# Order of the first loads, statistics ahead of the modulation, and the modulation on four column tiles, in a hybrid pool and state-space block

## The chip, the cores and the metric

The kernel runs on one core of a Trainium2 chip. The metric is the device time of one execution in microseconds. A core has five engines that run beside each other and meet at semaphores: TensorE (PE in the rows, its weight loads PEld), VectorE (DVE), ScalarE (ACT), GpSimd (POOL) and SyncE (SP), which issues most loads. ScalarE issues DMAs as well.

## The reference

One layer of a hybrid block with depth 1: 2048 latent tokens and 256 context tokens of width 1024. Both are normalised and modulated, projected by `w_in`, and fed to a pooling mixer and a bidirectional state-space mixer, whose outputs meet in `w_out`. Cut to what matters here:

```python
mod_lat = silu(c) @ w_ada + b_ada              # 1024 -> 3 x 1024
mod_ctx = silu(c_ctx) @ w_ada + b_ada
sh, sc, g = split(mod, 3)
hm = rmsnorm(h, norm_w) * (1 + sc) + sh        # for the context and for the latents
p  = hm @ w_in                                  # x/B/C columns, dt, gates, pool branch
# conv, chunked scans, box means, gates, then
h = h + g * (concat(y_pool, y_ssd) @ w_out);  out = rmsnorm(h, final_norm_w)
```

The pooling branch's per-group linear map (`pool_w`) is multiplied into its input projection: `s_wp` is that product, 256 x 1024 for each of four groups.

## The kernel before

Activations lie transposed, with channels on the 128 partitions and tokens along the free dimension: 8 chunks of channels, latents in four blocks of 512 tokens (`hm0` to `hm3`), the context in one of 256 (`hc`). Each is kept as a rounded part and a remainder, and each projection is three matmuls per chunk k (`project`).

The start of the program, up to line 460, is what the change touches. It does these things:

- *Modulation.* Eight chunks of `w_ada` (128 rows x 2048 columns, 1 MiB each, `ada`) are multiplied with `scol`, the silu of both condition vectors (2 columns per chunk): four matmuls of 128x2 by 128x512 per chunk into four banks `pm0` to `pm3`, two rows of each. Four copies (`mrow`), sixteen small transposes into `pmc`, and the bias give `mod` (shift and scale by channel) and `acol`, (1 + scale) times the norm's weight.
- *Statistics* (`Tokens.squares`, `mean`, `spread`). ScalarE squares eight chunks, GpSimd and VectorE add them up, TensorE sums over partitions (`ms`), a chain of small operations on VectorE and ScalarE forms the reciprocal root, ScalarE spreads it on a diagonal (`dg`), and TensorE makes a row block of it (`rstd`).
- *Modulation of the tokens* (`Tokens.modulate`). For each chunk VectorE forms `tt` (line 197), ScalarE the rounded part (line 199), VectorE the remainder (line 202), of `hc` for the context and `hm` for a latent block.
- *Pool maps* 0 and 1 (`pool_map`). TensorE forms eight pieces `pw`, ScalarE copies them, and issues two stores to `s_wp`.
- *Column tiles 0 and 1.* `pc` is the context's projection, `px` a latent block's, `pdt` the projection for dt. Weights come as `wraw_x`, are rounded by ScalarE (line 213), and the remainder is formed by GpSimd (line 214).

From column tile 2 on, a regular loop over 14 tiles follows, and then the other stages.

Three things set the order. Every engine works through its own list in order. A scheduler that works from estimated times makes these lists from the order of the program, so lines can move against each other. And each DMA, whichever engine issues it, takes the next of eight completion counters in turn (named DMAHW0 to DMAHW7 in the order's rows); an issue waits until the counter's previous DMA, the one eight places earlier, has landed. This wait stands in the list of the engine that issues.

Tiles with the tag `slot` share four large buffers: a fifth tile takes the buffer of one that is no longer read.

Of the kernel before, what the change touches and what calls it, by code (L numbers as in the profile page):

```python
# [23 lines left out]
def hybrid_block(ctx, tc, d, out):  # L24
    nc = tc.nc
    P = 128
# [24 lines left out]
    def mm(o, l, r, start, stop):  # L51
        nc.tensor.matmul(o, l, r, start=start, stop=stop)  # L52
# [28 lines left out]
    ident = const("ident", [P, P])  # L81
# [6 lines left out]
    mod = const("mod", [P, 16, 2])  # L88
    acol = const("acol", [P, 8, 2])
    scol = const("scol", [P, 8, 2])  # L90

    def exp_table(after):
        with tc.issue_after(after.ins):
            nc.scalar.preload_act_table_set("natural_log_exp_and_others")

    exp_table(nc.scalar.activation(scol, ccol, AF.Silu))

    def rsqrt(pool, ms, n, nm):
        v = pool.tile([P, n], F32, tag="rv", name=f"rv{nm}")
# [30 lines left out]
        return dg  # L130


    def ada_rows(ps, wa, k, who):

        for j, p in enumerate(ps):
            mm(p[0:who.stop - who.start, :], scol[:, k, who], wa[:, j * 512:(j + 1) * 512], k == 0, k == 7)

    class Tokens:

# [66 lines left out]
    def raw_weights(src, nm):  # L206
        raw = rpool.tile([P, 8, P], F32, tag="wraw", name=f"wraw_{nm}")
        nc.sync.dma_start(raw, src)
        return raw

    def split_weights(raw, nm, eng=nc.gpsimd):
        w = wpool.tile([P, 2, 8, P], F32R, tag="w", name=f"w_{nm}")
        nc.scalar.copy(w[:, 0], raw)
        eng.tensor_tensor(w[:, 1], raw, w[:, 0].bitcast(F32), op=ALU.subtract)
        return w
# [106 lines left out]
    wd = dp.tile([P, 8, P], F32R, tag="wd", name="wd")  # L322
    ctxt = Tokens(hc, 256, d["ctxT"], 1, "c", wpool.tile([P, 8, 256], F32, tag="w", name="xc"))
    ada = [slot(f"ada{a}", [P, 4, 2048], F32) for a in range(2)]
    cu = slot("cu", [P, 8192], F32)
    hm, tok = [], []

    def latent(b, raw=None):
        tok.append(Tokens(None, 512, d["xT"][b], 0, f"l{b}", raw, (4, 4, 6, 6)[b]))
        if raw is not None:  # L330
            tok[b].load()
# [2 lines left out]
        tok[b].h = slot(f"hm{b}", [P, 2, 8, 512], F32R)  # L334
        hm.append(tok[b].h)

    hm0 = slot("hm0", [P, 2, 8, 512], F32R)
    xs = slot("xs", [P, 2, 8, 512], F32)

    def pool_map(g, ks):  # L340
        uT = cu[:, 2048 * g:2048 * g + 2048].rearrange("p (a b) -> p a b", a=2)
        wl = cu[:, 4096 + 512 * g:4608 + 512 * g].rearrange("p (a b) -> p a b", a=2)
        wo = cu[:, 5120:7168] if g == 0 else cu[:, 0:2048]
        wo = wo.rearrange("p (k t) -> p k t", k=8)
        if 0 in ks:
# [15 lines left out]

    cols = [Columns(ct) for ct in range(16)]

    for k in range(4):
        load_ada(k)
    draw = rpool.tile([P, 8, 32], F32, tag="wraw", name="draw")
    nc.sync.dma_start(draw, d["w_dt"])
    ctxt.load()
    for k in range(4, 8):
        load_ada(k)  # L370
    norm_w = const("norm_w", [P, 8], d["norm_w"], pool=dp)
    b_mod = const("b_mod", [P, 16], d["b_mod"], pool=dp)
    conv_w = const("conv_w", [P, 16, 4], d["conv_w"], pool=dp)
    conv_b = const("conv_b", [P, 16], d["conv_b"], pool=dp)
    dtb_row = const("dtb_row", [P, 32], d["dt_bias"].broadcast_to([P, 32]), pool=dp)
    a_row = const("a_row", [P, 32], d["a_log"].broadcast_to([P, 32]), pool=dp)
    pool_map(0, (0,))
    latent(0, xs[:, 0])
    hm.append(hm0)
    tok[0].h = hm0  # L380
    raws = [raw_weights(d["w_xbc"][0], "x0")]
    pool_map(1, (0,))
    raws.append(raw_weights(d["w_xbc"][1], "x1"))
    nc.vector.memset(wd.bitcast(F32), 0.0)
    nc.vector.tensor_copy(wd[:, :, 0:32], draw)
    nc.vector.tensor_tensor(wd[:, :, 32:64], draw, wd[:, :, 0:32].bitcast(F32), op=ALU.subtract)
    pm = [pp(f"pm{j}") for j in range(4)]
    for k in range(6):
        ada_rows(pm, ada[k // 4][:, k % 4, :], k, slice(0, 2))
    for _ in ctxt.squares():  # L390
        pass
    for _ in ctxt.mean():
        pass
    for k in range(6, 8):
        ada_rows(pm, ada[k // 4][:, k % 4, :], k, slice(0, 2))
    ctxt.spread()
    latent(1, xs[:, 1])
    pmc = aux("pmc")
    pool_map(0, (1, 2))
    for j in range(4):  # L400
        mrow = sp.tile([2, 512], F32, tag="tt", bufs=3, name=f"mrow{j}")
        nc.vector.tensor_copy(mrow, pm[j][0:2, :])
        for i in range(4):
            q = 4 * j + i
            nc.tensor.transpose(pmc[:, 2 * q:2 * q + 2], mrow[:, i * P:(i + 1) * P], ident[0:2, 0:2])
    nc.vector.tensor_tensor(mod, pmc[:, 0:32].rearrange("p (a b) -> p a b", b=2),
                            b_mod.unsqueeze(2).broadcast_to([P, 16, 2]), op=ALU.add)
    nc.vector.scalar_tensor_tensor(acol, mod[:, 8:16, :], 1.0,
                                   norm_w.unsqueeze(2).broadcast_to([P, 8, 2]),
                                   op0=ALU.add, op1=ALU.mult)  # L410
    for _ in tok[0].squares():
        pass
    m = ctxt.modulate()
    maps = [(0, k) for k in range(3, 9)] + [(1, k) for k in range(1, 9)]

    def next_map():
        g, k = maps.pop(0)
        pool_map(g, (k,))

    for k in range(10):  # L420
        next(m)
        next_map()
        if k == 6:
            with tc.issue_after(tok[0].last.ins):
                cols[0].w = split_weights(raws[0], "x0")
    chain = tok[0].mean()
    for _ in range(3):
        next(chain, None)
    next_map()
    for _ in chain:  # L430
        pass
    next_map()
    next_map()
    tok[0].spread()
    next_map()
    cols[1].w = split_weights(raws[1], "x1")
# [392 lines left out]
    raws = {}  # L829
# [480 lines left out]
```

## Time and profile before

| | before |
|---|---|
| median of 3 runs | 1721.09 us (1718.83 to 1721.82) |
| the profiled execution, its time | 1716.81 us |
| its span | 1714.9 us |
| PE busy | 1663.5 us (97%), 8014 instructions |
| DVE busy | 1167.6 us (68%) |
| ACT busy | 790.4 us (46%) |
| POOL busy | 590.5 us (34%) |
| moved by DMA | 306.74 MB, 179 GB/s on average |

The profile is one execution, recorded instruction by instruction. Its time includes some 2 us around the span. Matmul ends are modelled, so a busy PE need not be one at its peak; starts of consecutive matmuls tell the pace.

### The profile page before, as it was taken

What the parts mean: (1) busy time and instruction counts of PE and PEld (TensorE: products, weight loads), DVE (VectorE), ACT (ScalarE), POOL (GpSimd) and SP (SyncE); (2) the same over time, 40 slices, a digit from 0 to 9 for tenths busy, and PEclk for the clock granted to TensorE, in tenths of its full rate; (3) what the DMA queues carried; (4) which work ended last, traced back from release to release, by engine and by line L of the source; (5) the groups of instructions that cost most, each with busy time, mean ns of one, the idle gap of its engine ahead of it and who ended that gap; (6) DMA issues with size and microseconds to landing.
All of it is one profiled execution on the core that took longest, in us unless ns stands there. A gap on an engine that the chain in (4) does not pass through costs nothing.

```text
span 1714.9 us, 24823 instructions
## 1 busy us (share of the span) xinstructions
PE 1663.5 (97%) x8014; PEld 1326.7 (77%) x8014; DVE 1167.6 (68%) x2456; ACT 790.4 (46%) x1929; POOL 590.5 (34%) x666
## 2 busy tenths in 40 slices
PE   8899999999999999999999999978999999999997
PEld 2778888888887888887877877756888888888886
DVE  1986544456665665665479898557788888888885
ACT  2753543443554444443411112355565556555663
POOL 1422110111215555555633334324333333333331
PEclk9999999999999999999999999988999999999999
DMA  9532233434444777778634456676666766676672
GB/s 374 176 122 69 72 104 89 130 107 133 138 140 139 257 251 251 253 244 295 209 120 146 136 160 196 185 220 193 179 197 193 214 192 197 194 212 190 202 194 83
DMA packets 209043, 306.74 MB, mean 179 GB/s; under 512 B 17937, under 2 KB 127377, under 8 KB 206610
## 3 DMA queue, kind: packets, MB, share of 16 engines
q1 hardware_dynamic: 115714, 219.43, 42.1%
q10 hardware_dynamic: 93200, 85.74, 14.8%
q8 instruction: 63, 1.03, 0.2%
q14 instruction: 66, 0.54, 0.1%
HBM read 207.81 MB, written 97.29 MB: 178 GB/s over the span
## 4 chain that ended last, share of the span: by engine, by line
PE 41%; DVE 8%; DMA 4%; ACT 1%; issue 1%; POOL 0%; SPq 0%; DVEq 0%; ACTq 0%; POOLq 0%
PE po L52 22%; PE yo L52 3%; PE pzp L52 3%; PE pv L52 3%; DVE bx L815 2%; PE y L966 2%; DVE bx L805 2%; PE pz L52 2%; PE y L972 2%; PE n L52 1%; PE cb L52 1%; DMA e<-s_rows 1%; DMA va<-s_v 1%; DVE bx L821 1%; PE ivationFunctionType.Copy L52 1%
## 5 line engine op out<-in xcount | busy, mean ns | idle before, releaser
L52 PE MATMUL px<-hm,w_x 128*128 128x512 f32 x1536 | 365.6, 397 | 2.4 <-ACT hm L199 1.3
L52 PEld LDWEIGHTS px<-hm,w_x 128*128 128x128 f32 x1536 | 288.2, 188 | 71.9 <-DVE hm L202 1.5
L52 PE MATMUL po<-wout,yp 128*128 128x512 f32 x768 | 212.2, 412 | 0.0
L52 PE MATMUL po<-wout,ys 128*128 128x512 f32 x768 | 211.2, 411 | 0.0
L258 DVE SCALAR_TENSOR_TENSOR cacc<-u,conv_w,cacc 128x512 f32<-128x512 f32 x168 | 138.2, 837 | 98.0 <-POOL u L308 56.3
L52 PE MATMUL pz<-hm,w_z 128*128 128x512 f32 x768 | 191.7, 399 | 1.5 <-ACT z L696 0.9
L52 PEld LDWEIGHTS pz<-hm,w_z 128*128 128x128 f32 x768 | 142.4, 188 | 35.3 <-ACT z L696 1.5
L52 PEld LDWEIGHTS po<-wout,yp 128*128 128x128 f32 x768 | 135.3, 189 | 34.6 <-issue 10.6
L52 PEld LDWEIGHTS po<-wout,ys 128*128 128x128 f32 x768 | 136.3, 190 | 23.7
L643 DVE TENSOR_TENSOR xw<-tkw,w_t 128x256 f32<-128x256 f32 x144 | 108.8, 795 | 43.4 <-ACT tkw L637 31.7
L953 POOL TENSOR_TENSOR yp<-yl,yp 128x256 fp32r<-128x256 f32 x64 | 50.3, 786 | 229.7 <-ACT yp L949 229.7
L650 POOL TENSOR_TENSOR xr<-xw,xh 128x512 fp32r<-128x512 f32 x72 | 96.6, 1342 | 70.2 <-ACT xh L648 68.8
L52 PE MATMUL pzp<-hm,w_q 128*128 128x512 f32 x384 | 95.2, 409 | 8.1 <-ACT va L782 8.1
L953 POOL TENSOR_TENSOR ys<-yg,ys 128x256 fp32r<-128x256 f32 x64 | 62.7, 979 | 116.6 <-ACT ys L949 58.9
L52 PE MATMUL ivationFunctionType.Copy<-hm,ivationFunctionType.Copy 128*128 128x512 f32 x384 | 100.5, 401 | 0.0
L52 PE MATMUL ivationFunctionType.Silu<-hm,ivationFunctionType.Silu 128*128 128x512 f32 x384 | 99.3, 401 | 0.0
L52 PEld LDWEIGHTS pzp<-hm,w_q 128*128 128x128 f32 x384 | 74.7, 196 | 27.9 <-ACT va L782 9.8
L52 PE MATMUL pv<-hm,w_v 128*128 128x512 f32 x384 | 91.2, 396 | 0.0
L648 ACT CAST xh<-xw 128x512 fp32r<-128x512 f32 x72 | 44.8, 622 | 99.6 <-DVE xw L643 98.1
L897 ACT ACTIVATE e<-e,nrb_t 128x128 f32<-128x128 f32 x256 | 81.1, 387 | 12.1 <-DMA e<-s_rows 12.1
L928 DVE SCALAR_TENSOR_TENSOR m<-cbl,dt_t,m 128x128 f32<-128x128 f32 x256 | 83.6, 389 | 3.6 <-ACT m L920 3.6
L52 PEld LDWEIGHTS pv<-hm,w_v 128*128 128x128 f32 x384 | 72.1, 188 | 17.5
(270 smaller groups left out, 3091.5 us busy)
## 6 DMA issues: line engine op xcount, KB each, us to landing
e<-s_rows SPq DMA_DIRECT2D x128, 256.0 KB, 5.1
s_tok<-tkw ACTq DMA_DIRECT2D x64, 384.0 KB, 3.0
bc<-s_bc SPq DMA_DIRECT2D x64, 256.0 KB, 4.1
tk<-s_tok SPq DMA_DIRECT2D x64, 256.0 KB, 5.9
st<-s_tok SPq DMA_DIRECT2D x64, 256.0 KB, 5.5
xl<-s_xs SPq DMA_DIRECT2D x72, 128.0 KB, 2.8
ada<-in_w_ada_dram SPq DMA_DIRECT2D x8, 1024.0 KB, 11.3
wraw_x<-in_w_xbc_dram SPq DMA_DIRECT2D x16, 512.0 KB, 4.8
```

The costliest lines, as they stand in the source:

```text
L52: nc.tensor.matmul(o, l, r, start=start, stop=stop)
L258: nc.vector.scalar_tensor_tensor(acc, u[:, k:k + n], conv_w[:, ct, k:k + 1], acc, op0=ALU.mult, op1=ALU.add)
L643: nc.vector.tensor_tensor(xw[:, s], h4(tk[:, 0, :]), w_t[:, s, c, 4 * g:4 * g + 4].unsqueeze(2).broadcast_to([P, 4, 64]), op=ALU.mult)
L648: nc.scalar.copy(xh, xw)
L650: nc.gpsimd.tensor_tensor(xr, xw, xh.bitcast(F32), op=ALU.subtract)
L805: nc.vector.tensor_tensor(dst, cur[:, 0:n, :], cur[:, step:step + n, :], op=ALU.add)
L815: nc.vector.tensor_tensor(dst, cur[:, :, 0:n], cur[:, :, step:step + n], op=ALU.add)
L897: nc.scalar.activation(s.e2[:, h, :], s.e2[:, h, :], AF.Identity, bias=nrb_t[:, s.c, 4 * s.g + h:4 * s.g + h + 1])
L928: nc.vector.scalar_tensor_tensor(s.m[:, h, :], s.cbl[:, 1, :], dt_t[:, 1, s.c, i:i + 1], s.m[:, h, :], op0=ALU.mult, op1=ALU.add)
L953: nc.gpsimd.tensor_tensor(y[:, 1], src, y[:, 0].bitcast(F32), op=ALU.subtract)
L966: nc.tensor.matmul(s.py[:, a * P:(a + 1) * P], src[:, a * P:(a + 1) * P], ident, start=(a, k) == (0, 0), stop=False, is_transpose=True, sk ...
L972: nc.tensor.matmul(o[64 * i:64 * i + 64, :], s.tk[:, 0, 64 * h:64 * h + 64], s.m[:, h, :], start=False, stop=True, skip_group_check=True)
```

## The change

The first loads come in another order: pool map 0, latent block 0, context and two small constants, then six chunks of `w_ada`, the dt weights, the first column tile's weights, the last two chunks, the second column tile's weights, pool map 1 and the remaining constants. The statistics of latent block 0 and of the context are written ahead of the modulation. The modulation uses 32 stationary columns (`srow`: two of them filled, the rest zero), and its four column blocks of 512 go to four column tiles of the array, so that they land in the four partition quarters of one bank `pm`. One copy and four transposes replace the four copies and sixteen transposes. Block 0's `hm0` is requested later in the program; its buffer is that of the second half of `w_ada`, as before.

```diff
+    srow = sp.tile([P, 8, 32], F32, tag="srow", bufs=1, name="srow")
+    nc.gpsimd.memset(srow, 0.0)
+    nc.vector.tensor_copy(srow[:, :, 0:2], scol)
...
-    def ada_rows(ps, wa, k, who):
-
-        for j, p in enumerate(ps):
-            mm(p[0:who.stop - who.start, :], scol[:, k, who], wa[:, j * 512:(j + 1) * 512], k == 0, k == 7)
+    def ada_rows(ps, wa, k):
+
+        for j in range(4):
+            nc.tensor.matmul(ps[32 * j:32 * j + 32, :], srow[:, k, :], wa[:, j * 512:(j + 1) * 512],
+                             start=k == 0, stop=k == 7, tile_position=(0, 32 * j), skip_group_check=True)
...
-    hm0 = slot("hm0", [P, 2, 8, 512], F32R)
     xs = slot("xs", [P, 2, 8, 512], F32)
...
-    for k in range(4):
+    pool_map(0, (0,))
+    latent(0, xs[:, 0])
+    ctxt.load()
+    norm_w = const("norm_w", [P, 8], d["norm_w"], pool=dp)
+    b_mod = const("b_mod", [P, 16], d["b_mod"], pool=dp)
+    for k in range(6):
         load_ada(k)
     draw = rpool.tile([P, 8, 32], F32, tag="wraw", name="draw")
     nc.sync.dma_start(draw, d["w_dt"])
-    ctxt.load()
-    for k in range(4, 8):
+    raws = [raw_weights(d["w_xbc"][0], "x0")]
+    for k in range(6, 8):
         load_ada(k)
...
+    raws.append(raw_weights(d["w_xbc"][1], "x1"))
+    pool_map(1, (0,))
...
+    for k in range(1, 9):
+        pool_map(0, (k,))
+    for _ in tok[0].squares():
+        pass
+    for _ in tok[0].mean():
+        pass
+    tok[0].spread()
     for _ in ctxt.squares():
         pass
     for _ in ctxt.mean():
         pass
-    for k in range(6, 8):
-        ada_rows(pm, ada[k // 4][:, k % 4, :], k, slice(0, 2))
     ctxt.spread()
...
+    pm = pp("pm")
+    for k in range(8):
+        ada_rows(pm, ada[k // 4][:, k % 4, :], k)
+        if k == 6:
+            cols[0].w = split_weights(raws[0], "x0")
     pmc = aux("pmc")
...
+    mrow = sp.tile([P, 512], F32, tag="tt", bufs=3, name="mrow")
+    nc.vector.tensor_copy(mrow, pm)
+    for i in range(4):
+        nc.tensor.transpose(pmc[:, i * P:(i + 1) * P], mrow[:, i * P:(i + 1) * P], ident)
...
+    cols[1].w = split_weights(raws[1], "x1")
+    hm.append(slot("hm0", [P, 2, 8, 512], F32R))
+    tok[0].h = hm[0]
     m = ctxt.modulate()
...
     for k in range(10):
         next(m)
...
+        if k > 1:
+            pool_map(1, (k - 1,))
+    latent(1, xs[:, 1])
```

What stands in the engines' lists after this. First the loads on SyncE of the changed kernel, from the first chunk of `w_ada` (`ada0` holds chunks 0 to 3, `ada1` chunks 4 to 7) to the second pool map's weights (the second `cu` row below), each with the counter that it waits for:

```order
L364 DMA ada0_117<-in_w_ada_dram 128x2048
L364 DMA ada0_117<-in_w_ada_dram 128x2048 [waits DMAHW0_49]
L364 DMA ada0_117<-in_w_ada_dram 128x2048 [waits DMAHW1_49]
L364 DMA ada0_117<-in_w_ada_dram 128x2048 [waits DMAHW2_49]
L364 DMA ada1_118<-in_w_ada_dram 128x2048 [waits DMAHW3_49]
L364 DMA ada1_118<-in_w_ada_dram 128x2048 [waits DMAHW4_49]
L376 DMA draw_135<-in_w_dt_dram 128x256 [waits DMAHW5_49]
L213 DMA wraw_x0_137<-in_w_xbc_dram 128x1024 [waits DMAHW6_49]
L364 DMA ada1_118<-in_w_ada_dram 128x2048 [waits DMAHW7_49]
L364 DMA ada1_118<-in_w_ada_dram 128x2048 [waits DMAHW0_49]
L350 DMA cu_119<-in_pool_w_dram 128x512 [waits DMAHW1_49]
L351 DMA cu_119<-in_w_uT_dram 128x2048 [waits DMAHW2_49]
```

The last chunk of `w_ada` uses counter 0, and the weights of pool map 1 use counter 1; behind them come the other counters in turn up to 7, with the second latent block, and then 0 and 1 again. These go to the two stores of pool map 0, in ScalarE's list of the changed kernel, which stand there behind the seventh of eight squares of latent block 0 and ahead of the last one and of the context's:

```order
L358 COPY cu_119<-pw0_7_181 128x256 [waits PE_49]
L166 ACTIVATE sq_l0_2_203<-xs_120 128x512 [waits DVE_49]
L361 DMA s_wp_70<-cu_119 1024x1x128 [waits DMAHW0_49,Activation_49]
L361 DMA s_wp_70<-cu_119 1024x1x128 [waits DMAHW1_49]
L166 ACTIVATE sq_l0_3_206<-xs_120 128x512 [waits DVE_49]
L166 ACTIVATE sq_c_7_237<-xc_116 128x256 [waits DMAHW4_49,Pool_49]
L166 ACTIVATE sq_c_1_242<-xc_116 128x256 [waits Pool_49]
```

Before, the same two stores wait for no counter (their list says only `[waits Activation_49]` for the first and nothing for the second), and stand behind all of the context's squares. The third place is TensorE's list of the changed kernel, behind the eight pieces of pool map 0 (the names: `pm` the modulation, `ms` the sum of squares, `rstd` the spread reciprocal root, of latent block 0 and of the context):

```order
L140 MATMUL pm<-ada_117,srow 32x512 x4
L52 MATMUL ms_l_210<-ones_100,sq_l0_0_192 128x1 x4
L140 MATMUL pm<-ada_117,srow 32x512 x8
L52 MATMUL rstd_l_233<-dgl_228,ones 128x512
L140 MATMUL pm<-ada_117,srow 32x512 x4
L52 MATMUL ms_c<-ones,sq_c_240 128x1 x2
L140 MATMUL pm<-ada_118,srow 32x512 x4
L52 MATMUL rstd_c<-dgc,ones 128x256
L140 MATMUL pm<-ada_118,srow 32x512 x12
L410 MATMUL pmc<-ident,mrow 128x128 x4
```

Before, six chunks of the modulation stood first, then `ms_c`, then the last two chunks and `rstd_c`; the sums of latent block 0 came behind the modulation. Later in this list, `pc1` (column tile 1, context) has two matmuls, then `pdt_c`, and six of block 0's `px`, before the sums of latent block 1 and the rest of `pc1`; `rstd` of blocks 1 and 2 stands at the end of the block before, where it was in its middle for block 1 and a little earlier for block 2. From the second half of block 2 on, TensorE's list is the same as before.

## Rows read from the trace of the kernel before

**Rows 1.** Stretches of the span: from, to and length in us, then busy us by engine.

```profile
6.50:37.20 30.70, 30.61 (x69) 6.21 (x70) 4.89 (x16) 4.22 (x13) 3.62 (x5) 1.00 0.98 393
37.20:67.50 30.30, 26.98 (x164) 23.09 (x164) 22.92 (x38) 23.22 (x56) 13.09 (x9) 1.00 0.85 314
67.50:138.30 70.80, 69.64 (x307) 55.36 (x308) 52.09 (x82) 40.55 (x76) 22.77 (x27) 0.98 0.29 97
138.30:1714.90 1576.60, 1536.25 (x7477) 1242.03 (x7475) 1086.39 (x2317) 719.68 (x1783) 550.35 (x621) 0.99 0.57 176
```

**Rows 2.** Groups by line, TensorE, 0 to 140 us: count, busy us, mean ns.

```profile
L52 PE MATMUL pm<-ada,scol 128*2 128x512 f32 x64 | 30.0, 630 | 6.6 <-DMA ada<-in_w_ada_dram 6.6
```

**Rows 3.** Timeline, all engines: start and length in us, instructions merged.

```profile
29.53 0.61 PE L52 MATMUL ms_c<-ones,sq_c 128*128 128x1 f32 x4
...
30.07 7.03 PE L52 MATMUL pm<-ada,scol 128*2 128x512 f32 x16
...
32.10 0.69 ACT L129 ACTIVATE dgc<-ident,rrc 128x128 f32<-128x128 f32 x2 [0.82 <-DVE rrc L123]
...
43.08 0.77 DVE L408 SCALAR_TENSOR_TENSOR acol<-mod,norm_w 128x16 f32<-128x16 f32 x1
...
58.80 2.08 PE L52 MATMUL pdt_c<-hc,wd 128*128 128x256 f32 x16
...
60.71 2.79 PE L52 MATMUL pc<-hc,w_x 128*128 128x256 f32 x22
...
67.60 0.73 PE L52 MATMUL px<-hm,w_x 128*128 128x512 f32 x2 [1.33 <-ACT hm L199]
...
69.63 2.93 PE L52 MATMUL px<-hm,w_x 128*128 128x512 f32 x6 [1.06 <-DVE hm L202]
...
138.27 0.40 PE L52 MATMUL pc<-hc,w_x 128*128 128x256 f32 x2
```

**Rows 4.** Timeline, SyncE's issues of loads.

```profile
1.18 2.34 SPq L360 DMA_DIRECT2D ada<-in_w_ada_dram  x4
...
11.44 0.33 SPq L45 DMA_DIRECT2D norm_w<-in_norm_w_dram  x1
...
26.90 0.33 SPq L347 DMA_DIRECT2D cu<-in_w_uT_dram  x1
```

**Rows 5.** Waits of SyncE, 0 to 130 us: us in total, times, longest.

```profile
SPq L45 <- DMA ada<-in_w_ada_dram: 8.6, 4, 2.2
```

**Rows 6.** Groups by line, VectorE, ScalarE and GpSimd, 0 to 140 us.

```profile
L202 DVE SCALAR_TENSOR_TENSOR hm<-tt_l,mod,hm 128x512 fp32r<-128x512 f32 x32 | 27.0, 871 | 1.0 <-ACT hm L199 0.7
L165 POOL TENSOR_TENSOR sq_l<-sq_l,sq_l 128x512 f32<-128x512 f32 x16 | 22.7, 1422 | 44.4 <-ACT sq_l L161 23.8 <-PE pw L52 20.4
...
L197 DVE SCALAR_TENSOR_TENSOR tt_l<-xs,acol,rstd_l 128x512 f32<-128x512 f32 x16 | 11.3, 739 | 0.5 <-PE rstd_l L52 0.5
...
L161 ACT ACTIVATE sq_l<-xs 128x512 f32<-128x512 f32 x16 | 9.5, 626 | 1.6 <-DVE sq_l L165 1.6
...
L165 DVE TENSOR_TENSOR sq_l<-sq_l,sq_l 128x512 f32<-128x512 f32 x8 | 7.9, 986 | 3.0 <-ACT sq_l L161 3.0
...
L202 DVE SCALAR_TENSOR_TENSOR hc<-tt_c,mod,hc 128x256 fp32r<-128x256 f32 x8 | 4.3, 553 | 0.4 <-ACT hc L199 0.4
...
L213 ACT CAST w_x<-wraw_x 128x1024 fp32r<-128x1024 f32 x4 | 4.2, 1046 | 0.0
...
L165 POOL TENSOR_TENSOR sq_c<-sq_c,sq_c 128x256 f32<-128x256 f32 x5 | 3.6, 723 | 17.2 <-ACT sq_c L161 16.9
L197 DVE SCALAR_TENSOR_TENSOR tt_c<-xc,acol,rstd_c 128x256 f32<-128x256 f32 x8 | 3.5, 475 | 0.1
...
L161 ACT ACTIVATE sq_c<-xc 128x256 f32<-128x256 f32 x8 | 2.9, 408 | 14.2 <-DMA xc<-in_ctxT_dram 12.9 <-POOL sq_c L165 1.3
...
L402 DVE COPY mrow<-pm 2x512 f32<-2x512 f32 x4 | 2.7, 678 | 4.9 <-PE pm L52 2.9 <-PE pmc L405 2.0
```

**Rows 7.** A stretch behind a gap of TensorE; third number from the end: granted clock.

```profile
70.00:72.00 2.00, 2.00 (x6) 1.52 (x6) 2.00 (x4) 0.50 (x2) 1.37 (x1) 0.50 0.00 0
```

More of the change, by code (lines that the diff above doesn't have):

```diff
@@ L367, in hybrid_block @@
     nc.sync.dma_start(draw, d["w_dt"])
-    ctxt.load()
-    for k in range(4, 8):
+    raws = [raw_weights(d["w_xbc"][0], "x0")]
+    for k in range(6, 8):
         load_ada(k)
-    norm_w = const("norm_w", [P, 8], d["norm_w"], pool=dp)
-    b_mod = const("b_mod", [P, 16], d["b_mod"], pool=dp)
+    raws.append(raw_weights(d["w_xbc"][1], "x1"))
+    pool_map(1, (0,))
     conv_w = const("conv_w", [P, 16, 4], d["conv_w"], pool=dp)
@@ L376, in hybrid_block @@
     a_row = const("a_row", [P, 32], d["a_log"].broadcast_to([P, 32]), pool=dp)
[L377 to L388, printed above, removed]
-        ada_rows(pm, ada[k // 4][:, k % 4, :], k, slice(0, 2))
+    for k in range(1, 9):
[5 more added lines that the diff above has]
+    tok[0].spread()
     for _ in ctxt.squares():
@@ L393, in hybrid_block @@
         pass
-    for k in range(6, 8):
-        ada_rows(pm, ada[k // 4][:, k % 4, :], k, slice(0, 2))
     ctxt.spread()
-    latent(1, xs[:, 1])
-    pmc = aux("pmc")
[L399 to L407, printed above, removed]
+    nc.vector.memset(wd.bitcast(F32), 0.0)
+    nc.vector.tensor_copy(wd[:, :, 0:32], draw)
+    nc.vector.tensor_tensor(wd[:, :, 32:64], draw, wd[:, :, 0:32].bitcast(F32), op=ALU.subtract)
+    pm = pp("pm")
[3 more added lines that the diff above has]
+            cols[0].w = split_weights(raws[0], "x0")
+    pmc = aux("pmc")
+    mrow = sp.tile([P, 512], F32, tag="tt", bufs=3, name="mrow")
+    nc.vector.tensor_copy(mrow, pm)
+    for i in range(4):
+        nc.tensor.transpose(pmc[:, i * P:(i + 1) * P], mrow[:, i * P:(i + 1) * P], ident)
+    nc.vector.tensor_tensor(mod.rearrange("p (j i) w -> p j i w", i=4),
+                            pmc.rearrange("p (i j w) -> p j i w", i=4, j=4)[:, :, :, 0:2],
+                            b_mod.rearrange("p (j i) -> p j i", i=4).unsqueeze(3).broadcast_to([P, 4, 4, 2]),
+                            op=ALU.add)
     nc.vector.scalar_tensor_tensor(acol, mod[:, 8:16, :], 1.0,
@@ L410, in hybrid_block @@
                                    op0=ALU.add, op1=ALU.mult)
-    for _ in tok[0].squares():
-        pass
+    cols[1].w = split_weights(raws[1], "x1")
+    hm.append(slot("hm0", [P, 2, 8, 512], F32R))
+    tok[0].h = hm[0]
     m = ctxt.modulate()
[L414 to L418, printed above, removed]
     for k in range(10):
         next(m)
[L422 to L436, printed above, removed]
+        if k > 1:
+            pool_map(1, (k - 1,))
+    latent(1, xs[:, 1])
     x2 = slot("x2", [P, 2, 8, 512], F32)
```

## The prediction

> **The bound.** I read the stretches of the span first [rows 1]. From 138.3 us on TensorE is busy for 1536 of 1577 us: what happens there is a dense chain of projections, so a microsecond won or lost before its start moves the end by the same. The change touches only the part before. There the reader is to see three stretches. In the first (6.5 to 37.2 us) TensorE does nothing but the modulation: 64 records, 30.0 us [rows 2], one every 0.434 us once it runs evenly (16 records between 30.07 and 37.02) [rows 3]. By that rhythm 64 would take 27.8 us; the other 2.2 us were lost in the first records, after TensorE had stood idle. A float32 matmul is two records, so one row chunk k of the weights (four column blocks) costs eight records, 3.47 us. In the second stretch VectorE and ScalarE are busy for 23 of 30 us each [rows 1]: statistics and modulation of context and latent block 0, with `acol` ready at 43.08 + 0.77 = 43.85 us [rows 3]. In the third, TensorE is dense from the first matmul on `hm` (67.60) to the first of column tile 2 (138.27), with 2.4 us idle near its start [rows 3].
>
> Then the loads. The last modulation chunk has landed at 26.9 us: the load of `uT` was held for it until then [rows 4, 5]. So TensorE, not the loads, ends the modulation before.
>
> **Loads.** The rate: `norm_w` was issued at 11.44 when chunk 2 had landed and `uT` at 26.90 when chunk 7 had [rows 4]; between lie 6.125 MiB, so 2.52 us per MiB, and the first three leave 11.44 - 3 x 2.52 = 3.88 us for the start. Now 0.25 (pool map), 1 (`uT`), 2 (latent), 1 (context), 6 (chunks 0 to 5), 0.125, 0.5 and 2 MiB stand up to chunk 7: 12.875 MiB, landing at 3.88 + 32.4 = 36.3 us, and the second pool map's weights 0.6 later, 36.9. Chunk 7 comes 9.4 us later than before.
>
> **The wait.** Every DMA uses one of eight completion counters in turn and its issue waits until the DMA eight places before it has landed. The trace shows such holds on SyncE: 8.6 us in four issues of small constants, each behind a chunk of `w_ada` [rows 5]. In the new order the two stores of pool map 0 (`s_wp`), which ScalarE issues, stand eight places behind chunk 7 and the second pool map's weights. ScalarE reaches them at about 18 to 19 us (latent landed at 3.88 + 3.25 x 2.52 = 12.1, then seven squares of 0.63 [rows 6] and five copies between them), and holds there until 36.9. With about 0.6 for the issue it goes on at 37.5. Behind the stores on ScalarE stand the last square of latent 0, all eight of the context, both `rsqrt` chains, and the cast of the first weights. The DMA page of the Trainium skill (DMA: Bandwidth & Descriptors, Anatomy of one DMA) says that DMA engines do not wait on semaphores and any such wait happens on the issuing sequencer; by that ScalarE stands still as SyncE does in the rows, and the forecast is the one below, while without it the sum would be that of the first rival.
>
> TensorE is caught too. Its order puts `ms_l0` behind chunk 0, and the chunks 1 to 7 behind `ms_l0`, `rstd_l0`, `ms_c` and `rstd_c`. So the chunks that have landed since 20 us wait for statistics that wait for chunk 7.
>
> **The chain.** From 37.5 us: the square 0.63, GpSimd's add 1.4 [rows 6], VectorE's last add 1.0 [rows 6], `ms_l0` with eight records at the rate of `ms_c` (four in 0.61 [rows 3]) 1.2: about 41.6. Its first matmul is at 40.4; the context's chain took 2.6 us from there (29.53) to the first diagonal copy (32.10) [rows 3], and with the longer `ms_l0`, a context square between (0.41 [rows 6]) and four copies instead of two (0.69 for two [rows 3]) the latent's is done at about 45.2. Two context squares stand behind it on ScalarE, then GpSimd's last two adds (0.72 each) and a short VectorE add [rows 6]: `ms_c` could start at 47.8, and `dgc` is done 3.3 us after its start.
>
> TensorE beside it: chunks 1 and 2, `rstd_l0`, chunk 3, `ms_c`, chunk 4, `rstd_c`, chunks 5 to 7. What a chunk costs on four column tiles no row shows. Ends: all four tiles side by side, two records, 0.87 us; all in a row, 3.47. I take half, 1.73: the two records of one float32 matmul use the same tile and the records of before follow each other evenly [rows 3], so I let only neighbours of different tiles overlap. Then: 41.6 + 2 x 1.73 + 2.2 for the slow first records = 47.3; `rstd_l0` 0.55, chunk 3 1.73: `ms_c` at 49.6, `dgc` 52.9, `rstd_c` 53.4, chunks 5 to 7 58.6. All side by side: `ms_c` 47.8, `dgc` 51.1, end 54.3. In a row: end 69.7.
>
> The Trainium skill (TensorEngine Tiling (Array Packing), Theoretical Speedup) gives up to four times for four tiles of 32 columns; as an estimate by that page the chunk is 0.87 us and the forecast 4 us shorter. No row here shows it.
>
> One copy of `pm` (0.68 [rows 6], for 16 matmul pieces in four copies before), four transposes of 128 columns (about 1.0, nearest to `ms_c`'s four records), `mod` and `acol` (0.77 [rows 3]) and the hand-overs: 3.1 us. So `acol` is ready at 61.7 instead of 43.85: +17.8 us (13.6 side by side, 28.9 in a row).
>
> **After `acol`.** The next part goes to column tile 2. Before: 138.27 - 43.85 = 94.4 us. Now the squares of latent 0 and pool map 0 are already done, but pool map 1, the squares of latent 1 and both modulations follow on VectorE and ScalarE, and the cast of weights 1 stands on ScalarE behind `hm0`'s sixth piece. TensorE has only two matmuls of `pc1` before it and nothing else to go on with. VectorE up to that piece: eight `tt_c` and eight `hc` (0.475 + 0.553), six `tt_l` (0.74), four `hm` (0.87), three adds (0.99, often 0.7) [rows 6], some 18 us; ScalarE's piece and the cast (1.05 [rows 6]) make it 20. Then TensorE still owes `pc1` and `pdt_c` (40 matmuls at 0.12 [rows 3]: 4.9), `ms_l1` 0.9, and the third stretch: 70.7 us less its 2.4 idle and the 1.7 lost to a clock at 0.50 to 0.85 for some us behind that gap (0.50 in 70 to 72 [rows 7]): 66.6. New gaps: `rstd_l1` and `rstd_l2` now stand at the end of the preceding block, so the first `hm` piece of the next one (three `tt_l` and one `hm`, 3.1 us [rows 6]) is covered by little; 0.5 and 1.8 us. The idle time before the cast costs a slow clock as before, 1.7. Sum 20 + 4.9 + 0.9 + 66.6 + 2.3 + 1.7 = 96.4: +2.0 us (-2 without the new gaps and the slow clock, +4 if `hm` pieces are late as well).
>
> Nothing: the memset and copy of `srow` lie before the first chunk has landed; fewer matmul records of `pmc` and `mrow` copies are counted above.
>
> **Sum.** 17.8 + 2.0 = +19.8 us. The profiled execution took 1716.8 us (span 1714.9); 1736.6 for one like it. The median of the runs is 1721.1, 4.3 above it, so 1741.
>
> **Rivals.** *ScalarE isn't held, and the new order does its work.* Against it: the eight-place wait in the program's order, shown on SyncE [rows 5]. For it: no row of before shows such a hold on ScalarE. Then the statistics would be ready some 19 us earlier, by 33; chunk 7 lands at 36.3 plus 2.5 for 1 MiB of stores between, its last chunk 1.7 and 3.1 lead to `acol` at 43.6, -0.2, and with +2.0 it comes to 1723, no change to be measured. The point: ScalarE must pass the stores by about 19.5 us, since the chain from there to the end of chunk 7 takes 21 and chunk 7 would end at 40.5.
>
> *The column tiles run one behind the other.* Eight records per chunk as before; 1741 + 11 = 1752.
>
> *They run side by side*: 1741 - 4 = 1737; it counts with the forecast.
>
> *The later stages take some of it back.* The 40 us that TensorE stands idle behind 138.3 [rows 1] would have to be waits for something that doesn't move with the start. Loads and stores there follow the engines, so I see little: 1741 less 10 at most.
>
> **Numbers.** Held ScalarE with overlapping tiles 0.68; held with tiles in a row 0.18; some given back 0.08; not held 0.06. The likeliest is 1741. The range goes from tiles side by side with the lower end of the second term (1741 - 4 - 4) to tiles in a row with all else as forecast (1752): 1733 to 1753, and leaves out the not-held case and parts of two others. This kernel's measurement can tell about 0.2%, 3.4 us. Faster by more 0.02, within it 0.04, slower 0.94.
>
> **Signs.** ScalarE idle from about 19 to 37 us, ended by a DMA; TensorE idle from the end of chunk 0 to about 40; `ms_l0` at 40.5, `acol` ready near 62, the cast of weights 1 near 82, the first matmul of column tile 2 near 158, and from there the same distance to the end. Chunks of `pm` about 1.7 us apart when they follow each other. Wrong would be: squares of the context before 30 us; `acol` near 44; or the distance from the first matmul of column tile 2 to the end changed by more than 2 us.

## The result, and the profile after

The changed kernel takes 1737.29 us (median of 5 runs, 1732.04 to 1742.13), the kernel before on the same chip 1721.09 (5 runs, 1718.83 to 1721.82). The ratio is 1.0096, with a 95% interval of 1.0071 to 1.0121: slower by about 1%. The profiled execution took 1734.49 us with a span of 1732.6, against 1716.81 and 1714.9 before: 17.7 us more. The forecast was 1741, in a range of 1733 to 1753.

Four stretches of the span as in [rows 1], but with the second ending at 67.6 and not at 67.5, now of the changed kernel (from, to, length in us; busy us of PE, PEld, DVE, ACT and POOL with their instructions; PEclk, DMA share, GB/s):

```profile
6.50:37.20 30.70, 10.43 (x40) 7.76 (x40) 2.19 (x3) 6.12 (x15) 2.54 (x2) 0.74 1.01 419
37.20:67.60 30.40, 22.14 (x108) 10.99 (x108) 15.14 (x45) 14.32 (x39) 7.37 (x8) 0.81 0.63 223
67.60:138.30 70.70, 63.27 (x305) 51.99 (x306) 50.95 (x80) 42.54 (x84) 23.95 (x26) 0.95 0.28 87
138.30:1714.90 1576.60, 1544.55 (x7514) 1248.38 (x7513) 1084.65 (x2304) 722.33 (x1778) 559.79 (x624) 0.99 0.57 176
```

In the first stretch the transfers run at 419 GB/s, but TensorE is busy for 10.4 us instead of 30.6. VectorE and ScalarE do little there, as before (2.2 and 6.1 us, 4.9 and 4.2 before), though the change moves the statistics up into this stretch; in the second one, too, they are busy for 15 and 14 us instead of 23. Their work comes later, and TensorE is busy for 8 us more behind 138.3 us. The timeline of ScalarE shows why (start and length in us, instructions merged; in brackets the idle time before and what ended it):

```profile
16.50 0.67 ACT L166 ACTIVATE sq_l<-xs 128x512 f32<-128x512 f32 x1
36.13 1.30 ACTq L361 DMA_DIRECT2D s_wp<-cu  x2
37.48 0.63 ACT L166 ACTIVATE sq_l<-xs 128x512 f32<-128x512 f32 x1 [20.30 <-DMA cu<-in_pool_w_dram]
...
45.30 1.28 ACT L133 ACTIVATE dgl<-ident,rrl 128x128 f32<-128x128 f32 x4 [1.31 <-DVE rrl L127]
```

From 17.2 to 36.1 us ScalarE stands in front of the two stores of pool map 0. The first store was issued at 36.13, when the load that its counter stood for, the last chunk of `w_ada`, had landed. The next square runs at 37.48, behind the second store; the bracket names the later of the two loads, the second pool map's weights. The square reads neither. The view of ScalarE's waits up to 40 us (us in total, times, longest) counts it as one wait of 20.3 us:

```profile
ACT sq_l L166 <- DMA cu<-in_pool_w_dram: 20.3, 1, 20.3
```

TensorE in the same timeline, with one line of VectorE, `acol`, and one of ScalarE, the cast of weights 1; the last line is the first matmul of column tile 2, which answers to the last one of [rows 3]:

```profile
17.09 1.07 PE L140 MATMUL pm<-ada,srow 128*32 128x512 f32 x8 [1.01 <-DMA ada<-in_w_ada_dram]
...
40.29 1.87 PE L52 MATMUL ms_l<-ones,sq_l 128*128 128x1 f32 x8 [22.14 <-DVE sq_l L178]
...
42.09 3.51 PE L140 MATMUL pm<-ada,srow 128*32 128x512 f32 x16
46.62 1.12 PE L52 MATMUL rstd_l<-dgl,ones 128*128 128x512 f32 x2 [1.02 <-ACT dgl L133]
47.68 1.06 PE L140 MATMUL pm<-ada,srow 128*32 128x512 f32 x8
49.07 0.61 PE L52 MATMUL ms_c<-ones,sq_c 128*128 128x1 f32 x4 [0.33 <-DVE sq_c L178]
...
52.39 1.22 PE L52 MATMUL rstd_c<-dgc,ones 128*128 128x256 f32 x2 [1.71 <-ACT dgc L133]
53.54 3.77 PE L140 MATMUL pm<-ada,srow 128*32 128x512 f32 x24
...
58.22 0.63 PE L410 MATMUL pmc<-ident,mrow 128*128 128x128 f32 x4 [0.92 <-DVE mrow L408]
...
59.11 0.17 DVE L415 SCALAR_TENSOR_TENSOR acol<-mod,norm_w 128x16 f32<-128x16 f32 x1
...
76.30 1.03 ACT L218 CAST w_x<-wraw_x 128x1024 fp32r<-128x1024 f32 x1
...
77.38 0.80 PE L52 MATMUL pc<-hc,w_x 128*128 128x256 f32 x2 [6.50 <-ACT w_x L218]
...
154.81 0.40 PE L52 MATMUL pc<-hc,w_x 128*128 128x256 f32 x2
```

The reader is to see three things. TensorE did chunk 0 at 17.09 and then nothing for 22 us, though chunks 1 to 6 landed in that time; it goes on when the statistics do. `acol` is ready at 59.11 + 0.17 = 59.28 instead of 43.85, 15.4 us later. And column tile 2 starts at 154.81 instead of 138.27, 16.5 us later; from there to the end of the span it is 1577.8 us against 1576.6, so 1.2 of the 17.7 us lie behind it.

### The profile page after: what moved, and what is told of

The parts are those of the page before. It is cut to its first block, busy times and chain, and to the rows that moved or that the text cites. A ratio compares the mean times of both kernels' runs of the same rounds, so it can differ in the third digit from the quotient of the medians.

```text
span 1732.6 us, 24799 instructions
## 1 busy us (share of the span) xinstructions
PE 1649.4 (95%) x8002; PEld 1326.0 (77%) x8002; DVE 1161.1 (67%) x2454; ACT 791.2 (46%) x1929; POOL 595.4 (34%) x667
## 4 chain that ended last, share of the span: by engine, by line
PE 37%; DVE 10%; DMA 3%; ACT 1%; issue 1%; SPq 0%; DVEq 0%; ACTq 0%
PE po L52 21%; DVE bx L795 3%; DVE bx L805 3%; PE yo L52 3%; PE y L956 2%; PE y L962 2%; PE pz L52 2%; PE n L52 1%; PE pzp L52 1%; PE pv L52 1%; DVE bx L811 1%; PE cb L52 1%; DMA e<-s_rows 1%; DMA va<-s_v 1%; DVE bx L810 1%
## 6 DMA issues: line engine op xcount, KB each, us to landing
ada<-in_w_ada_dram SPq DMA_DIRECT2D x8, 1024.0 KB, 15.9
```

## The experiments

Each ran beside the kernel before on the same chip, and its ratio is against that one (whose medians there were 1717.9 to 1718.4 us). The first two columns of times are read from the timeline of each profiled execution; the time of a single execution differs by several us between repetitions of one kernel (1714.7 to 1723.3 in 33 of the kernel before), so the ratio decides on the total, and the start of column tile 2 on where the time went.

| kernel | `acol` ready | column tile 2 starts | median us | ratio, 95% interval |
|---|---|---|---|---|
| before | 43.85 | 138.27 | 1721.09 | 1 |
| changed | 59.28 | 154.81 | 1737.29 | 1.0096 [1.0071, 1.0121] |
| stores behind `dgc` | 40.75 | 138.95 | 1717.68 | 0.9998 [0.9987, 1.0009] |
| stores on SyncE | 40.73 | 136.81 | 1716.41 | 0.9989 [0.9981, 0.9998] |
| chunks ahead of statistics | 62.43 | 147.84 | 1726.96 | 1.0048 [1.0035, 1.0061] |
| change without tiles | 76.39 | 164.05 | 1742.64 | 1.0134 [1.0119, 1.0148] |
| before with tiles | 31.41 | 135.27 | 1714.34 | 0.9972 [0.9961, 0.9983] |
| SyncE, `pdt_c` first | 41.10 | 139.14 | 1719.97 | 1.0009 [0.9998, 1.0019] |
| pool maps behind | 36.18 | 133.12 | 1713.49 | 0.9977 [0.9967, 0.9988] |
| the same, `pdt_c` first | 38.13 | 134.89 | 1714.73 | 0.9979 [0.9967, 0.9991] |
| pool maps behind, in turn | 36.60 | 134.72 | 1713.81 | 0.9981 [0.9971, 0.9991] |
| tiles, latent earlier | 30.84 | 134.87 | 1714.54 | 0.9986 [0.9977, 0.9995] |

**The stores behind the statistics.** The two stores of pool map 0 get a function of their own, and are issued behind the last diagonal copy of the context:

```diff
-                for a in range(2):
-                    nc.scalar.dma_start(s_wp[2 * g + a], wo[:, :, a * P:(a + 1) * P])
...
     ctxt.spread()
+    with tc.issue_after(ctxt.dg_last.ins):
+        store_map(0, cu[:, 5120:7168].rearrange("p (k t) -> p k t", k=8))
```

> The changed kernel with one thing moved: the two stores of pool map 0 are issued on ScalarE behind the last diagonal copy of the context (dgc) instead of ahead of the last square of latent 0. Loads, their order, the tiles and the other engines' work stay. Theory (the stores' wait for chunk 7 holds ScalarE, and with it the statistics and the chunks on TensorE): no idle time of ScalarE from 16.5 to 36 us; the statistics run 20 us earlier, ms_l0 at about 20, rstd_c by about 33; only chunk 7, landed at 36.1, is left, and acol is ready near 40.4 instead of 59.28; the median falls by about 19 us, to 1716 to 1721. Rival (the hold is not what costs: the later landing of chunk 7 and a long chain of statistics do, with or without it): acol near 57 or later, the median 1734 or more. Between them, 1722 to 1733, would mean that some other wait takes over half of the hold.

Measured: 1717.68 us, ratio 0.9998 to the kernel before, so about 1% under the changed kernel. From its timeline (all engines, as above):

```profile
20.84 1.27 PE L52 MATMUL ms_l<-ones,sq_l 128*128 128x1 f32 x8 [2.53 <-DVE sq_l L178]
...
33.48 5.29 PE L140 MATMUL pm<-ada,srow 128*32 128x512 f32 x24
...
36.87 4.06 ACTq L364 DMA_DIRECT2D s_wp<-cu  x2
...
40.58 0.17 DVE L420 SCALAR_TENSOR_TENSOR acol<-mod,norm_w 128x16 f32<-128x16 f32 x1
...
42.10 2.35 POOL L219 TENSOR_TENSOR w_x<-wraw_x,w_x 128x1024 fp32r<-128x1024 f32 x1 [13.59 <-ACT w_x L218]
42.18 2.30 DVE L507 TENSOR_SCALAR a_row<-a_row 128x32 f32<-128x32 f32 x1 [1.43 <-ACT a_row L493]
44.40 1.25 DVE L202 SCALAR_TENSOR_TENSOR tt_c<-xc,acol,rstd_c 128x256 f32<-128x256 f32 x3
...
138.95 0.40 PE L52 MATMUL pc<-hc,w_x 128*128 128x256 f32 x2
```

The same loads in the same order, the same tiles, and `ms_l0` stands at 20.84 instead of 40.29. `acol` is ready at 40.75, 18.5 us earlier, with 40.4 expected: the theory holds and its rival (`acol` near 57) falls. The stores still wait (issued from 36.87 on), but nothing of the statistics is behind them now. Something is: the cast of weights 0 and `a_row`, and so the first `tt_c`, which runs 3.65 us after `acol` (for the 2.30 us of `a_row` see the last section).

**The stores on SyncE.** One line; no other engine's order changes:

```diff
-                    nc.scalar.dma_start(s_wp[2 * g + a], wo[:, :, a * P:(a + 1) * P])
+                    (nc.scalar if g else nc.sync).dma_start(s_wp[2 * g + a], wo[:, :, a * P:(a + 1) * P])
```

> The changed kernel with one thing altered: the two stores of pool map 0 are issued by SyncE, behind the loads, instead of by ScalarE; every other engine keeps its order, and the stores wait for the same counters. Theory (what cost was that the wait stood on ScalarE): SyncE takes the hold, with nothing of the start behind it but two later loads; acol is ready near 40.7 as with the stores issued behind dgc, and what that run then lost (3.55 us from acol to the first tt_c, because ScalarE was still at the stores, the cast of weights 0 came behind them, and GpSimd's subtraction of weights 0 and a_row fell between) is not lost; first matmul of column tile 2 near 135.4, the median 1713 to 1716. Rival (a_row's load lands behind the second uT, at about 40.5, and VectorE's a_row operation stands ahead of the first tt_c anyway): no gain over the run with the stores behind dgc, 1717 to 1719.

Measured: 1716.41 us, ratio 0.9989. SyncE, VectorE, ScalarE and TensorE in its timeline:

```profile
35.92 7.28 SPq L361 DMA_DIRECT2D s_wp<-cu  x2
...
40.56 0.17 DVE L415 SCALAR_TENSOR_TENSOR acol<-mod,norm_w 128x16 f32<-128x16 f32 x1
...
41.31 0.23 ACT L488 ACTIVATE a_row<-a_row 128x32 f32<-128x32 f32 x1 [6.71 <-DMA a_row<-in_a_log_dram]
41.58 0.18 DVE L502 TENSOR_SCALAR a_row<-a_row 128x32 f32<-128x32 f32 x1 [0.84 <-ACT a_row L488]
...
136.81 0.40 PE L52 MATMUL pc<-hc,w_x 128*128 128x256 f32 x2
```

The stores now wait on SyncE and are issued from 35.92 on; of the start's chain nothing stands behind them there. The median lies between the two forecasts. The first `tt_c` follows `acol` after 0.9 us instead of 3.65, and column tile 2 starts 2.1 us earlier than with the stores behind `dgc`; more was expected (3.55), and a part that stayed is the wait for the load of `a_row`, which its rival named: VectorE stands idle for 0.84 us before `a_row`, until ScalarE's part of it, which waited for that load. With the queue that issues two stores as the one thing altered, column tile 2 starts 18.0 us earlier than in the changed kernel. That isolates the cause.

**The chunks ahead of the statistics.** The loop over the chunks is written between the squares and the means, and `ms_l0` is issued behind the last chunk; ScalarE stays held:

```diff
+    with tc.issue_after(pm_last.ins):
+        chain = tok[0].mean()
+        next(chain)
+    for _ in chain:
+        pass
```

> The changed kernel with TensorE's order changed: all eight chunks of pm ahead of ms_l0 and the statistics' other matmuls; ScalarE is still held by the two stores, the loads stay. The scheduler also puts pool map 1 between the statistics. Theory (of the 15.4 us by which acol is late, a part is TensorE's: chunks 1 to 7 stand behind matmuls of the statistics): the chunks end by about 38.5, the statistics follow ScalarE's release at 37.5 and end with rstd_c near 50, acol is no longer the last; the start of column tile 2 moves from 154.8 to about 146, the median to 1727 to 1731. Rival (the hold of ScalarE is everything, and the chunks lie beside the statistics): start of column tile 2 above 152, the median 1735 or more.

Measured: 1726.96 us, ratio 1.0048, column tile 2 at 147.84. TensorE and VectorE:

```profile
36.34 1.94 PE L140 MATMUL pm<-ada,srow 128*32 128x512 f32 x8 [0.58 <-DMA ada<-in_w_ada_dram]
...
40.54 1.87 PE L52 MATMUL ms_l<-ones,sq_l 128*128 128x1 f32 x8 [2.27 <-DVE sq_l L179]
...
62.26 0.17 DVE L419 SCALAR_TENSOR_TENSOR acol<-mod,norm_w 128x16 f32<-128x16 f32 x1
...
147.84 0.40 PE L52 MATMUL pc<-hc,w_x 128*128 128x256 f32 x2
```

The total is about as expected, the way is only partly: the statistics were to end near 50, and `rstd_c` stands at 59.92. The last chunk ends at 38.3, and `ms_l0` stands at 40.5 as in the changed kernel. But the scheduler put the transposes behind `rstd_c` and pool map 1 with the squares of latent 1 between the statistics; so `acol` came later than in the changed kernel (62.43), and column tile 2 still 7 us earlier, because work that had stood behind `acol` was done. The run shows that the order on TensorE and ScalarE under a held ScalarE is worth 7 of the 16.5 us. It doesn't show how much of that is the chunks' own.

**The change without the tiles.** Modulation as before (two columns of `scol`, four banks), all else as in the change:

```diff
-    pm = pp("pm")
+    pm = [pp(f"pm{j}") for j in range(4)]
...
-        ada_rows(pm, ada[k // 4][:, k % 4, :], k)
+        ada_rows(pm, ada[k // 4][:, k % 4, :], k, slice(0, 2))
```

> The changed kernel with the modulation as it was before: two columns of scol, four PSUM banks, one matmul per column block and row chunk, sixteen transposes of two columns; the load order, the stores and the statistics stay as in the change. Theory (four tiles run nearly side by side, about 1.06 us for a chunk against 3.47 in the kernel before): chunks 1, 2 and 3 and 5 to 7 lie on the chain, 2.4 us each, chunk 4 is partly covered, and the four copies of pm add 1 to 3; acol comes 15 to 18 us later than 59.28, the median is 1752 to 1756. Rival (the chunks are covered by the statistics, and the tiles are worth little here): acol by 64, the median 1738 to 1742.

Measured: 1742.64 us, ratio 1.0134, 0.6 us above the rival's span and 9 below the theory's. TensorE, VectorE and ScalarE:

```profile
42.51 8.95 PE L52 MATMUL pm<-ada,scol 128*2 128x512 f32 x16
...
75.91 0.48 DVE L414 SCALAR_TENSOR_TENSOR acol<-mod,norm_w 128x16 f32<-128x16 f32 x1
...
86.13 1.03 ACT L217 CAST w_x<-wraw_x 128x1024 fp32r<-128x1024 f32 x1
...
164.05 0.40 PE L52 MATMUL pc<-hc,w_x 128*128 128x256 f32 x2
```

Up to `acol` the theory holds: two chunks take 8.95 us instead of 3.51, and `acol` comes 17.1 us later than with tiles (15 to 18 expected). The step that failed was to carry this to the end one for one: column tile 2 starts only 9.2 us later. The scheduler gave ScalarE another order; the cast of weights 1 stands 9.7 us behind `acol` (86.13 less 76.39) instead of 17.0 (76.30 in the changed kernel), and TensorE's idle time of 6.5 us before it is gone. That this is all of the 7.9 us is argued, not shown.

**The tiles alone in the kernel before.** `ada_rows`, `srow`, `mrow` and the transposes of the change, all loads and statistics as before:

```diff
-    pm = [pp(f"pm{j}") for j in range(4)]
+    pm = pp("pm")
...
-        ada_rows(pm, ada[k // 4][:, k % 4, :], k, slice(0, 2))
+        ada_rows(pm, ada[k // 4][:, k % 4, :], k)
```

> The kernel before with only the modulation on four column tiles; its load order and the order of its statistics stay. Theory (TensorE ended the modulation before, at 37.0, ten us behind the last chunk's landing at 26.9): the chunks now follow the loads, the modulation ends by about 29 and acol is ready by 33; the latent, which lands near 34.5, is the next thing waited for, where ScalarE took its squares up at 40.3 before; so the start moves by about 6 us and the median is 1713 to 1717. Rival (ScalarE and VectorE bound the second stretch anyway, or the latent's statistics do): the gain is under 2 us, 1719 to 1722.

Measured: 1714.34 us, ratio 0.9972, inside the expected span. TensorE, VectorE and ScalarE:

```profile
27.04 1.93 PE L140 MATMUL pm<-ada,srow 128*32 128x512 f32 x8 [0.41 <-DMA ada<-in_w_ada_dram]
...
31.24 0.17 DVE L413 SCALAR_TENSOR_TENSOR acol<-mod,norm_w 128x16 f32<-128x16 f32 x1
...
38.18 2.19 ACT L166 ACTIVATE sq_l<-xs 128x512 f32<-128x512 f32 x4 [0.71 <-DMA xs<-in_xT_dram]
...
135.27 0.40 PE L52 MATMUL pc<-hc,w_x 128*128 128x256 f32 x2
```

And where the squares began in the kernel before:

```profile
40.29 2.19 ACT L161 ACTIVATE sq_l<-xs 128x512 f32<-128x512 f32 x4
```

Most chunks now wait for their load, `acol` is ready 12.4 us earlier than before, and 3.0 us of that reach column tile 2, where about 6 were expected: the squares of the latent wait for its load until 38.18 (34.5 expected) instead of starting at 40.29. So the tiles are the part of the change that gains, and the new order of loads was not needed for it: with the hold taken away, tiles and new order together come to 0.9989, no better than the tiles alone.

**`pdt_c` ahead of `pc1`**, to fill TensorE's wait for the cast of weights 1, on top of the stores on SyncE:

```diff
     cols[0].context()
-    cols[1].context()
     pdts = [project_dt(hc, 256, 16, "c")]
     next(pdts[0])
+    cols[1].context()
```

> As the run before it with the stores on SyncE, and pdt_c written ahead of pc1, so that TensorE has 16 matmuls to do while it waits for the cast of weights 1 (6.5 us idle in the changed kernel, at 71 to 77). Theory (that wait is on the path that sets the start of column tile 2): 3.3 to 5 us less than the run before it, the median 1709 to 1712. Rival (VectorE, which makes the hm pieces of all four blocks at nearly TensorE's rate, is the bound of that stretch): the idle time moves to px_1 or px_2 and the median stays within 1.5 us of the run before it.

Measured: 1719.97 us, ratio 1.0009, 3.6 us slower than the run it builds on, where the rival allowed 1.5. TensorE:

```profile
52.89 2.08 PE L52 MATMUL pdt_c<-hc,wd 128*128 128x256 f32 x16
59.57 0.80 PE L52 MATMUL pc<-hc,w_x 128*128 128x256 f32 x2 [4.60 <-ACT w_x L218]
...
86.44 2.92 PE L52 MATMUL px<-hm,w_x 128*128 128x512 f32 x6 [1.98 <-DVE hm L207]
...
139.14 0.40 PE L52 MATMUL pc<-hc,w_x 128*128 128x256 f32 x2
```

The rival holds in its mechanism. The idle time before `pc1` shrinks to 4.60, and a new one of 1.98 stands at `px_1`, which waits for VectorE; the six matmuls behind it take 2.92 us instead of 1.56, at a granted clock of 0.50 (1.2 GHz) instead of 1.00, and VectorE is busy for all of these 2.92 us. A wait of TensorE in a stretch that VectorE bounds is no reserve.

**The pool maps behind the modulation's weights.** Pool map 0 is loaded next to pool map 1, and both are computed during the modulation of the context:

```diff
-    pool_map(0, (0,))
     latent(0, xs[:, 0])
...
+    pool_map(0, (0,))
     pool_map(1, (0,))
...
-    for k in range(1, 9):
-        pool_map(0, (k,))
...
+        if k < 8:
+            pool_map(0, (k + 1,))
```

> The changed kernel with pool map 0's weights loaded behind the modulation's, next to pool map 1's, and its matmuls and copies in the modulation of the context, beside pool map 1's; so no store stands on ScalarE in the start, and chunk 7 lands 1.25 MiB earlier. Theory (acol follows chunk 7 once ScalarE is free): chunk 7 lands near 33.2, acol is ready near 37.9; the eight further copies add 2.8 us to ScalarE behind it; first matmul of column tile 2 near 135, the median 1712 to 1716. Rival (TensorE and ScalarE wait for the two uT, which land at 36.3 and 39.5, and the copies stand ahead of hc and hm pieces): column tile 2 no earlier than 139, the median 1718 or more.

Measured: 1713.49 us, ratio 0.9977, `acol` ready at 36.18 and column tile 2 at 133.12, both a little earlier than expected. In this kernel, and in the next, pool map 1's copies overwrite a part of pool map 0's weights that is still to be read, so that a part of pool map 0's result is another one; the times are those of the same instructions in this order.

> As the run with the pool maps behind, and pdt_c written ahead of pc1. Theory: again 3 to 5 us less than that run if the wait for the cast of weights 1 is on the path, the median 1708 to 1713. Rival: within 1.5 us of it if VectorE bounds that stretch.

Measured: 1714.73 us, column tile 2 at 134.89: no gain again. The run that this one builds on, with the pool maps behind, has no wait of TensorE for the cast of weights 1, in the view of its waits from 30 to 140 us, so there was none to fill.

> As the run with both pool maps behind, but with pool map 1's matmuls and copies behind all of pool map 0's (in that run pool map 1's copies overwrote a part of pool map 0's weights while they were still needed, so that a part of pool map 0's result was another one). Theory (no store stands on ScalarE in the start, chunk 7 lands 1.25 MiB earlier, the statistics are ready before it): acol near 36.2 as there, first matmul of column tile 2 at 133 to 136, the median 1712 to 1716, faster than the kernel before by 0.15 to 0.35 per cent. Rival (pool map 1's copies and the stores, now later on ScalarE, hold hm0's pieces and the cast of weights 1): column tile 2 at 137 or later, the median 1717 or more.

This one computes the whole reference again: sixteen maps in turn, two for each step of the modulation.

```diff
+    maps = [(g, k) for g in range(2) for k in range(1, 9)]
     for k in range(10):
         next(m)
-        if k > 1:
-            pool_map(1, (k - 1,))
+        for g, i in maps[2 * k - 4:2 * k - 2] if k > 1 else ():
+            pool_map(g, (i,))
```

Measured: 1713.81 us, ratio 0.9981, inside the expected span; faster than the kernel before by 0.1 to 0.3%, and than the changed one by about 1.1% (0.9981 over 1.0096). TensorE and VectorE:

```profile
36.43 0.17 DVE L413 SCALAR_TENSOR_TENSOR acol<-mod,norm_w 128x16 f32<-128x16 f32 x1
...
134.72 0.40 PE L52 MATMUL pc<-hc,w_x 128*128 128x256 f32 x2
```

**The tiles and an earlier latent in the kernel before**: `latent(0, xs[:, 0])` one line up, ahead of `pool_map(0, (0,))`.

> The kernel before with the modulation on four column tiles, and latent 0 loaded ahead of pool map 0's weights. Theory (with the tiles alone, ScalarE waited for latent 0 until 38.2 and the first matmul on hm0 stood at 65.5): latent 0 lands 1.25 MiB, about 3 us, earlier, and the chain through ms_l0 and rstd_l0 with it; first matmul of column tile 2 at 132 to 133.5 instead of 135.3, the median 1711 to 1713. Rival (both uT and ScalarE's sixteen copies, now behind the latent, are waited for instead): no gain over the tiles alone, 1713.5 to 1716.

Measured: 1714.54 us, ratio 0.9986, column tile 2 at 134.87. ScalarE takes up the squares at 32.9 instead of 38.2, and nothing comes of it: the matmuls and copies of both pool maps now stand behind them, `pc0` starts at 57.6, and the first matmul on `hm0` at 66.3 (65.5 with the tiles alone). The rival holds.

## Why the prediction was right, and by how much it was off

*Loads.* Chunk 7 was worked out to land at 36.3 us and the second pool map's weights at 36.9. The first store was issued at 36.13 and the square behind the second ran at 37.48 (37.5 forecast). The rate from [rows 4] carried over.

*The wait.* ScalarE reached the stores at 17.2 (18 to 19 forecast) and was held to the place forecast. Two runs that change only the place or the queue of the stores take 15.9 and 18.0 us off the start of column tile 2. The rule of the Trainium skill quoted for this (DMA: Bandwidth & Descriptors, Anatomy of one DMA: the semaphore wait is the issuing sequencer's) agrees with both traces: the sequencer that issues is the one that stands, ScalarE in one, SyncE in the other.

*TensorE caught at `ms_l0`.* As forecast: `ms_l0` at 40.29 (40.4), `ms_c` at 49.07 (49.6), `rstd_c` behind `dgc` at 52.39 (52.9).

*The chain to `acol`: +15.4 us, +17.8 forecast. This is the term that was mis-sized*, by two of its parts. A chunk on four tiles was taken as 1.73 us, half way between 0.87 (side by side) and 3.47 (in a row). It took 1.06 alone at the full clock, against 3.47 before, and 3.51 for two and 3.77 for three in a row at a clock of 0.54 and 0.73 in those stretches. At about half clock (0.52) three follow each other in 5.29 us (33.48 in the run with the stores behind `dgc`), 1.76 each, twice 0.88: the tiles do run side by side, and what is left above 0.87 is the clock and the last records. So the sign "about 1.7 us apart" came true by luck: the clock made it so, not a partial overlap. The Trainium skill (TensorEngine Tiling (Array Packing), Theoretical Speedup) gives up to four times for tiles of 32 columns; 3.47 against 0.88 agrees. The argument that only neighbours of different tiles overlap was wrong. And from the end of `pm` to `acol` it took 2.0 us (57.31 to 59.28) instead of 3.1, with `acol` itself 0.17 instead of the 0.77 of [rows 3], which it took beside an addition of GpSimd (last section). In the other direction `ms_l0` took 1.87 at half clock instead of 1.2. The forecast named the case side by side, with +13.6 and 1737, as its lower one. That the median is 1737.29 is in part luck: that case comes to +15.6 us (13.6 + 2.0) for the profiled execution, and +17.7 was measured.

*After `acol`: +1.1 us up to column tile 2, +2.0 forecast.* The cast of weights 1 stood at 76.3 to 77.3, 18 us behind `acol` and not 20; of the new gaps at the first `hm` pieces there was none at `px_1` and 0.8 us in two at `px_2`, where 2.3 were forecast; 1.2 us were added behind column tile 2, where nothing was. The stretch is near to a constant only while the scheduler keeps its order: 94.4 and 95.5 in the two kernels, but 85.4 to 104.0 in the runs of the table.

*The sum.* +19.8 forecast for the profiled execution, +17.7 measured; the rest of the difference to 1741 is the median, which stands 2.8 us above the profiled execution here and 4.3 before.

*The rivals.* Tiles in a row falls by the chunk. ScalarE not held falls by its idle time of 20.3 us. The run nearest to what that case would be worth, the stores on SyncE, takes 0.9989 of the kernel before and not the 1.0011 (1723) worked out: there the stores' transfer doesn't stand ahead of chunk 7 (2.5 us of the estimate), and the last chunk and the way to `acol` are shorter. Later stages gave nothing back.

## What to carry to other kernels

When a load or store changes its place in the program, follow the completion counters as well as the data: a store that nobody waits for can hold the engine that issues it until an unrelated load eight places ahead has landed, and with it all compute queued there; SyncE, with nothing urgent behind, is the place for it. A matmul with few columns on the stationary side can be worth packing into column tiles, here for -0.28% alone, since four ran in about the time of one. A measured distance from a gate such as `acol` to the next landmark is no constant: whatever doesn't depend on the gate can be moved across it, and whether it is, an automatic scheduler decides anew after each edit.

## What the runs showed of the hardware that was not expected

*A small VectorE instruction can last as long as a large GpSimd one.* `a_row` (128x32 elements) took 0.18 us on VectorE in the run with the stores on SyncE, and 2.30 us, 42.18 to 44.48, in the run with the stores behind `dgc`, where GpSimd's subtraction of weights 0 ran from 42.10 to 44.45. In the changed kernel that subtraction fell at 53.34, with VectorE idle. `acol` of the kernel before is a second case: it took 0.77 us there, 43.08 to 43.85, beside an addition of GpSimd that ended at 43.82, and 0.17 in the changed kernel, where GpSimd was idle.

```profile
42.55 1.27 POOL L165 TENSOR_TENSOR sq_l<-sq_l,sq_l 128x512 f32<-128x512 f32 x1 [20.42 <-PE pw L52]
```

The Trainium skill (SBUF — State Buffer, SBUF: two separate sides) says that VectorE instructions with two SBUF inputs, or in a two-port mode, compete with GpSimd for one pair of SBUF ports, which whichever starts first holds for its whole instruction while the other is blocked. The ends, 0.03 us apart in both cases, agree with it, and no run here separates it from other causes.

*TensorE ran at half clock while it followed the loads.* With the tiles alone in the kernel before, TensorE waited before most of its chunks, for up to 3.4 us, and from 14 to 29 us its granted clock was 0.50 (1.2 of 2.4 GHz); a chunk took 1.93 us there instead of 1.06. In the kernel before it was busy all through that stretch, at a granted clock of 1.00. From, to and length, then busy us by engine and the granted clock, with the tiles alone and before:

```profile
14.00:29.00 15.00, 10.57 (x45) 2.03 (x45) 2.95 (x13) 4.22 (x13) 3.62 (x5) 0.50 0.95 367
14.00:29.00 15.00, 15.00 (x36) 2.96 (x35) 1.57 (x4) 3.12 (x9) 3.62 (x5) 1.00 0.94 361
```

The next load came 2.5 us after the one before, so the slow clock cost little: some 0.9 us, in the last chunk.
